# A two-layer encoder trunk on one core: the first norm's weights spread by a product with ones, and products that nobody reads ahead of the first real ones

## The chip, the core and the metric

The kernel runs on one core of a Trainium2 chip. A core has five engines that work side by side, each through its own queue and strictly in the order of that queue: TensorE (PE in the profile; its weight loads are shown as PEld), VectorE (DVE), ScalarE (ACT), GpSimd (POOL) and SyncE (SP, which here only issues DMAs). They wait for each other through semaphores. Matrix products read SBUF, the on-chip memory of 128 partitions, and write PSUM, from which VectorE or ScalarE take the results.

The metric is the device time of one execution, in microseconds (us); lower is better.

## What is computed

A float32 input of 512 tokens by 1024 features passes through two layers. Each layer is a token mixer and a channel mixer (a GeGLU network with a short convolution), each between two RMS norms:

```python
def rms_norm(x, g):
    xf = x.astype(jnp.float32)
    y = xf * lax.rsqrt(jnp.mean(xf * xf, axis=-1, keepdims=True) + EPS)
    return (y * g.astype(jnp.float32)).astype(x.dtype)
...
    for layer in range(DEPTH):
        i = layer // 2
        hn = rms_norm(x, norm_mix_pre[layer])
        if layer % 2 == 0:
            m = retention_na_mixer(hn, ab_w_in[i], ...)
        else:
            m = ssd_mixer(hn, c_w_in[i], ...)
        x = x + rms_norm(m, norm_mix_post[layer])
        f = conv_geglu_ffn(rms_norm(x, norm_ffn_pre[layer]), ...)
        x = x + rms_norm(f, norm_ffn_post[layer])
```

The change touches only the very first step, `rms_norm(x, norm_mix_pre[0])`, and what stands around it. The weights of that norm, `g`, are one row of 1024 numbers; the kernel needs them in every one of the 128 partitions.

## The kernel before

The 512 tokens are four tiles of 128 partitions (`t` = 0 to 3). The kernel is written with a framework that keeps pools of buffers, puts in the waits, and chooses each engine's order of instructions from the data dependences and from priorities; an engine then works its list off strictly in that order. So the place of an instruction in its engine's list matters as much as its inputs.

Start of the program (`trunk`): SP issues the loads of the four tiles of x (512 KB each), between them the load of the norm's weights and the first weight units of the mixer. The norm's weights come by `bcast` (L71): one DMA that writes the row of 4 KB into all 128 partitions, 512 KB in SBUF, called `gain`. Then for each tile t:

- `norm` (L113): ScalarE squares and sums the tile (`sumsq`, L110, written `junk`), VectorE adds the epsilon (`v_x`, L100), GpSimd raises to the power -1/2 (`r_x`, L102), and VectorE multiplies x by this and by `gain`, in two halves of 512 features (`xs`, L122).
- `turn` (L125): TensorE transposes each half in four products with the identity into one PSUM tile (`pt`, L131), and `split` (L77) takes it apart into a rounded part and the rest: ScalarE writes `xh` (L79), VectorE writes `xl` (L80).

Every product in the kernel is done as three (`mm3`, L82): rounded by rounded (L84), and the two cross terms with a rest (L85, L86). Weights are treated alike: `wunit` (L54) issues the load of a unit of 128 x 1024 into `wst` (two buffers), and `split` writes its rounded part `whi` on ScalarE (L79) and its rest `wlo` on VectorE (L80) into three buffers each. These splits are given a high priority, by which the framework places them early.

The first consumer, at the head of `mixer0`, is a projection: eight weight units, of which the first four make the first half; each unit serves two 128-row blocks of the contraction for each of the four token tiles, so one half has 4 x 4 x 2 x 3 = 96 products. The first product needs `xh` of tile 0 and the first `whi`; the second (L85) needs `xl` as well, the third (L86) `wlo`.

```python
                for t in range(NT):
                    tt = slice(t * P, (t + 1) * P)
                    for i in range(2):
                        k = 2 * u + i
                        E.mm3(ps[t], E.xh[:, k, tt], E.xl[:, k, tt], *w[i], k == 0, k == KD - 1)
```

PSUM has two pools of four tiles: `mm` for the sums of the projections, `px` for everything else, the transposes among it. A pool `tmp` of seven buffers holds, among others, `xs`.

Of the kernel before, what the change touches and what calls it, by code (L numbers as in the profile page):

```python
# [7 lines left out]
F32 = mybir.dt.float32  # L8
# [7 lines left out]
P = 128  # L16
S = 512
NT = S // P
D = 1024
# [6 lines left out]
class Env:  # L26


    def __init__(self, ctx, tc):
        self.tc, self.nc = tc, tc.nc  # L30
        nc = self.nc
        pool = lambda name, bufs, **kw: ctx.enter_context(tc.tile_pool(name=name, bufs=bufs, **kw))
        self.const = pool("const", 1)
        self.res = pool("res", 1)
        self.wst = pool("wst", 2)
        self.whi = pool("whi", 3)
        self.wlo = pool("wlo", 3)
        self.gain = pool("gain", 2)
        self.tmp = pool("tmp", 7)
        self.small = pool("small", 6)  # L40
        self.mm = pool("mm", 4, space=PSUM)
        self.px = pool("px", 4, space=PSUM)
        self.dram = pool("dram", 1, space=DRAM)

        self.ident = self.const.tile([P, P], F32, name="ident")
        make_identity(nc, self.ident)
        self.mhalf = self.const.tile([P, 1], F32, name="mhalf")
        nc.vector.memset(self.mhalf, -0.5)
        self.x = self.res.tile([P, NT, D], F32, name="x")
        self.xh = self.res.tile([P, KD, S], R32, name="xh")  # L50
        self.xl = self.res.tile([P, KD, S], R32, name="xl")
        self.late, self.xs = [], {}

    def wunit(self, src, parts=None):  # L54


        nc = self.nc
        st = self.wst.tile([P, 1024], F32, name="wst")
        nc.sync.dma_start(st, src)
        halves = slice(0, 512), slice(512, 1024)  # L60
        if parts is None:
            hi, lo = self.whi.tile([P, 1024], R32, name="whi"), self.wlo.tile([P, 1024], R32, name="wlo")
            with self.tc.high_priority(60):
                self.split(hi, lo, st)
            return [(hi[:, c], lo[:, c]) for c in halves]
        with self.tc.high_priority(60):
            for j, c in enumerate(halves):
                self.split(parts[j], parts[j + 2], st[:, c])
        return [(parts[j], parts[j + 2]) for j in range(2)]
# [789 lines left out]
def trunk(tc, x, norms, ab, ssd, ffns, out):  # L859

    nc = tc.nc
    with ExitStack() as ctx:
        E = Env(ctx, tc)
        w0 = []
        for t in range(NT):
            nc.sync.dma_start(E.x[:, t, :], x[t * P:(t + 1) * P])
            if t == 0:
                g0 = E.bcast(norms[0, 0])
            else:
                w0.append(E.wunit(ab[0][0, len(w0)]))  # L870
        for t in range(NT):
            E.norm(t, g0)
            E.turn(t)

        def then(row):
            g = []

            def done(t):
                if not g:
                    g.append(E.bcast(row))  # L880
                E.norm(t, g[0])
            return done

        def store(t):
            E.xs.pop(t, None)
            for h in range(2):
                c = slice(h * 512, h * 512 + 512)
                nc.sync.dma_start(out[t * P:(t + 1) * P, c], E.x[:, t, c])

        mixer0(E, w0, *ab, norms[0, 1], then(norms[0, 2]))  # L890
        ffn(E, *ffns[0], norms[0, 3], then(norms[1, 0]))
        mixer1(E, *ssd, norms[1, 1], then(norms[1, 2]))
        ffn(E, *ffns[1], norms[1, 3], store)
        E.flush()
# [80 lines left out]
def build(tc, ap, out):  # L975
    trunk(
        tc, ap["x"], ap["norms"],
        [ap["ab_" + n] for n in ("v", "fm", "rot", "dist", "logit", "gn", "bias", "out")],
        [ap["c_" + n] for n in ("dt", "fm", "cw", "dtc", "cols", "mask", "out")],
        [[ap[f"f{l}_{n}"] for n in ("up", "cw", "down")] for l in range(2)],  # L980
        out,
    )
# [18 lines left out]
```

## Time and profile before

| | us |
|---|---|
| median of 3 runs (lowest to highest) | 1478.65 (1475.88 to 1478.84) |
| time of the profiled execution | 1481.63 |
| its span, first to last instruction | 1479.9 |
| PE busy in it | 1445.4 (98%) |
| PEld busy | 1150.1 (78%) |
| DVE busy | 954.7 (65%) |
| ACT busy | 721.8 (49%) |
| POOL busy | 61.5 (4%) |

The profiled execution moved 166.34 MB by DMA, a mean of 112 GB/s. The mean granted TensorE clock of the span was 0.991 of full speed. Times in views are counted from the first instruction. A row of the timeline gives the start, the duration, the engine, the line of the program, the operation, the tile written and the tiles read, how many equal instructions are merged, and in brackets how long the engine was idle before and what ended that. Durations of neighbours on one engine overlap a little, since an instruction starts while the one ahead of it drains; the distance of two starts is what one of them costs in a row of many.

### The profile page before, as it was taken

What the parts mean: (1) busy time and instruction counts of PE and PEld (TensorE: products, weight loads), DVE (VectorE), ACT (ScalarE), POOL (GpSimd) and SP (SyncE); (2) the same over time, 40 slices, a digit from 0 to 9 for tenths busy, and PEclk for the clock granted to TensorE, in tenths of its full rate; (3) what the DMA queues carried; (4) which work ended last, traced back from release to release, by engine and by line L of the source; (5) the groups of instructions that cost most, each with busy time, mean ns of one, the idle gap of its engine ahead of it and who ended that gap; (6) DMA issues with size and microseconds to landing.
All of it is one profiled execution on the core that took longest, in us unless ns stands there. A gap on an engine that the chain in (4) does not pass through costs nothing.

```text
span 1479.9 us, 18034 instructions
## 1 busy us (share of the span) xinstructions
PE 1445.4 (98%) x6848; PEld 1150.1 (78%) x6848; DVE 954.7 (65%) x1484; ACT 721.8 (49%) x1186; POOL 61.5 (4%) x66
## 2 busy tenths in 40 slices
PE   7999999999999999999999999999899999999998
PEld 6866656788888888888778787777778888888886
DVE  7367668676665663236889886899887656654133
ACT  4345546445444442225688677567645444443121
POOL 0010100010000000001000000000020000000000
PEclk9999999999999999999999999999999999999999
DMA  7442132233333332242366355255532332333232
GB/s 247 150 129 77 51 100 65 74 101 93 92 101 100 92 101 84 93 127 98 110 176 202 107 164 160 70 151 155 173 111 86 100 100 89 100 97 100 85 100 85
DMA packets 56950, 166.34 MB, mean 112 GB/s; under 512 B 7200, under 2 KB 7968, under 8 KB 56864
## 3 DMA queue, kind: packets, MB, share of 16 engines
q1 hardware_dynamic: 56864, 165.20, 36.2%
q8 instruction: 54, 0.88, 0.2%
q14 instruction: 32, 0.26, 0.1%
HBM read 157.57 MB, written 5.51 MB: 110 GB/s over the span
## 4 chain that ended last, share of the span: by engine, by line
PE 82%; DVE 7%; DMA 4%; ACT 3%; issue 2%; POOL 1%; SPq 0%; DVEq 0%; POOLq 0%; ACTq 0%
PE mm L84 24%; PE mm L86 24%; PE mm L85 24%; DMA pb<-pd 2%; PE y L423 2%; DVE wlo L80 1%; DVE xf L654 1%; PE st L690 1%; PE sc L413 1%; PE pi L734 1%; PE pt L131 1%; DMA wst<-in_c_fm 1%; PE sc L412 1%; PE sc L458 1%; DMA wst<-in_c_out 1%
## 5 line engine op out<-in xcount | busy, mean ns | idle before, releaser
L84 PE MATMUL mm<-xh,whi 128*128 128x512 f32 (+2 forms) x1216 | 466.8, 384 | 2.4 <-DVE xf L654 1.4
L85 PE MATMUL mm<-xh,wlo 128*128 128x512 f32 (+2 forms) x1216 | 465.1, 383 | 0.7 <-DVE wlo L80 0.7
L86 PE MATMUL mm<-xl,whi 128*128 128x512 f32 (+2 forms) x1216 | 465.2, 383 | 0.0
L80 DVE TENSOR_TENSOR wlo<-wst,whi 128x1024 fp32r<-128x1024 f32 (+1 forms) x214 | 263.8, 1234 | 222.7 <-ACT whi L79 222.3
L79 ACT CAST whi<-wst 128x1024 fp32r<-128x1024 f32 (+1 forms) x214 | 223.4, 1044 | 218.4 <-PE mm L85 160.4
L84 PEld LDWEIGHTS mm<-xh,whi 128*128 128x128 f32 (+1 forms) x1216 | 229.3, 189 | 51.0 <-issue 4.1
L86 PEld LDWEIGHTS mm<-xl,whi 128*128 128x128 f32 (+1 forms) x1216 | 228.8, 188 | 47.3 <-issue 3.4
L85 PEld LDWEIGHTS mm<-xh,wlo 128*128 128x128 f32 (+1 forms) x1216 | 229.6, 189 | 45.4 <-issue 1.7
L216 DVE SCALAR_TENSOR_TENSOR cv<-mm,cwt,cv 128x511 f32<-128x511 f32 x88 | 65.7, 747 | 94.9 <-ACT cv L215 94.9
L84 PE MATMUL mm<-whi,hh 128*128 128x512 f32 x320 | 126.4, 395 | 0.0
L85 PE MATMUL mm<-whi,hl 128*128 128x512 f32 x320 | 126.3, 395 | 0.0
L86 PE MATMUL mm<-wlo,hh 128*128 128x512 f32 x320 | 126.3, 395 | 0.0
L215 ACT ACTIVATE cv<-mm,cwt 128x512 f32<-128x512 f32 x88 | 68.5, 778 | 38.1 <-PE mm L86 37.9
L79 ACT CAST hh<-cv 128x512 fp32r<-128x512 f32 x44 | 27.3, 621 | 100.2 <-DVE cv L224 100.0
L86 PEld LDWEIGHTS mm<-wlo,hh 128*128 128x128 f32 x320 | 60.3, 188 | 14.2
L85 PEld LDWEIGHTS mm<-whi,hl 128*128 128x128 f32 x320 | 60.3, 188 | 14.0
L84 PEld LDWEIGHTS mm<-whi,hh 128*128 128x128 f32 x320 | 60.3, 188 | 13.8
L222 ACT ACTIVATE cv<-cv 128x512 f32<-128x512 f32 x44 | 27.8, 632 | 86.3 <-DVE cv L217 86.3
L217 DVE SCALAR_TENSOR_TENSOR cv<-mm,cwt,cv 128x511 f32<-128x511 f32 x88 | 66.0, 750 | 3.0
L715 ACT ACTIVATE ds<-um,tok,ddt 128x128 f32<-128x128 f32 x128 | 55.7, 484 | 16.7 <-DVE e L718 16.3
L712 ACT ACTIVATE e<-pb,tok 128x128 f32<-128x128 f32 x128 | 42.8, 392 | 14.1 <-DMA pb<-pd 13.8
L654 DVE SCALAR_TENSOR_TENSOR xf<-mm,cwt,xf 128x510 f32<-128x510 f32 (+1 forms) x64 | 47.3, 742 | 3.5 <-ACT xf L651 3.4
(232 smaller groups left out, 1898.5 us busy)
## 6 DMA issues: line engine op xcount, KB each, us to landing
wst<-in_f_up SPq DMA_DIRECT2D x88, 512.0 KB
wst<-in_f_down SPq DMA_DIRECT2D x44, 512.0 KB
wst<-in_c_fm SPq DMA_DIRECT2D x40, 512.0 KB
pb<-pd SPq DMA_DIRECT2D x64, 256.0 KB
wst<-in_ab_fm SPq DMA_DIRECT2D x20, 512.0 KB
gain<-yd SPq DMA_DIRECT2D x32, 256.0 KB
wst<-in_c_out SPq DMA_DIRECT2D x16, 512.0 KB
gain<-in_norms SPq DMA_DIRECT2D x8, 512.0 KB
```

What stands on the lines that cost most here:

```text
L79: self.nc.scalar.copy(hi, src)
L80: self.nc.vector.tensor_tensor(lo, src, hi.bitcast(F32), op=ALU.subtract)
L84: mm(out, lh, rh, start=first, stop=False)
L85: mm(out, ll, rh, start=False, stop=False)
L86: mm(out, lh, rl, start=False, stop=last)
L215: nc.scalar.activation(o, ps, AF.Identity, scale=w(1), bias=w(3))
L216: nc.vector.scalar_tensor_tensor(o[:, 1:], ps[:, :S - 1], w(0), o[:, 1:], op0=ALU.mult, op1=ALU.add)
L217: nc.vector.scalar_tensor_tensor(o[:, :S - 1], ps[:, 1:], w(2), o[:, :S - 1], op0=ALU.mult, op1=ALU.add)
L423: nc.tensor.matmul(o["ry"][h * 64:h * 64 + 64], rv[:, i, c:c + 64], o["sd", i][h], start=i == 0, stop=i == NT - 1)
L654: nc.vector.scalar_tensor_tensor(r[:, a], ps[:, b], wc(j), r[:, a], op0=ALU.mult, op1=ALU.add)
L712: nc.scalar.activation(e[:, c], pb[0][:, cc], AF.Identity, scale=-1.0, bias=tok[:, 0, c, h:h + 1])
L715: nc.scalar.activation(ds[:, c], um, AF.Identity, scale=ddt[:, c, h:h + 1], bias=tok[:, 1, c, H + h:H + h + 1])
```

## The change

```diff
+    def lead_in(self, row):
+        nc = self.nc
+        one = self.const.tile([1, P], F32, name="one")
+        nc.vector.memset(one, 1.0)
+        src = [self.tmp.tile([1, 512], F32, name="row", tag="tmp") for _ in range(2)]
+        for h in range(2):
+            nc.sync.dma_start(src[h], row.rearrange("(o d) -> o d", o=1)[:, h * 512:h * 512 + 512])
+        idle = self.px.tile([P, P], F32, name="idle", tag="px")
+        for _ in range(8):
+            nc.tensor.matmul(idle, self.ident, self.ident, start=True, stop=True)
+        g = self.gain.tile([P, D], F32, name="gain")
+        for h in range(2):
+            c = slice(h * 512, h * 512 + 512)
+            ps = self.px.tile([P, 512], F32, name="pg", tag="px")
+            nc.tensor.matmul(ps, one, src[h], start=True, stop=True)
+            nc.scalar.copy(g[:, c], ps)
+        for _ in range(6):
+            nc.tensor.matmul(idle, self.ident, self.ident, start=True, stop=True)
+        return g
...
         w0 = []
+        g0 = E.lead_in(norms[0, 0])
         for t in range(NT):
             nc.sync.dma_start(E.x[:, t, :], x[t * P:(t + 1) * P])
-            if t == 0:
-                g0 = E.bcast(norms[0, 0])
-            else:
+            if t > 0:
                 w0.append(E.wunit(ab[0][0, len(w0)]))
```

The row of weights is now loaded into one partition, in two DMAs of 2 KB. A product of a column of ones with it (`pg`, one for each half) writes the row into all 128 partitions of PSUM, and ScalarE copies the two halves into `gain`. Ahead of these two products stand eight products of the identity with itself, behind them six, into a PSUM tile `idle` that is never read. All sixteen are plain float32 products. The 512 KB broadcast DMA is gone. The other norms of the kernel still use `bcast`.

The framework then orders all instructions anew. Line numbers of the program move by 22 (L79 becomes L101, L122 becomes L144). Behind the first projection every engine's list is as before; at the start it is not. The first rows of ScalarE's list, before (`junk` with `ssx` is the sum of squares, one instruction for each tile):

```order
L110 ACT_TABLE_LOAD
L110 ACTIVATE junk,ssx<-x 128x1024 x2
L79 CAST whi<-wst 128x1024
L79 CAST xh<-pt 128x4x128 x2
L110 ACTIVATE junk,ssx<-x 128x1024
L79 CAST whi<-wst 128x1024
```

and of the change:

```order
L132 ACT_TABLE_LOAD
L132 ACTIVATE junk,ssx<-x 128x1024
L101 CAST whi<-wst 128x1024 x2
L71 COPY gain<-pg 128x512 x2
L132 ACTIVATE junk,ssx<-x 128x1024
L101 CAST whi<-wst 128x1024
L101 CAST xh<-pt 128x4x128 x3
```

The two copies that make `gain` stand behind the casts of the first two weight units, and the sum of squares of the second tile stands behind those copies.

VectorE's list from its first work on x, before:

```order
L100 TENSOR_SCALAR v_x<-ssx 128x1
L122 SCALAR_TENSOR_TENSOR xs<-x,r_x,gain 128x512 x2
L100 TENSOR_SCALAR v_x<-ssx 128x1
L122 SCALAR_TENSOR_TENSOR xs<-x,r_x,gain 128x512 x2
L80 TENSOR_TENSOR wlo<-wst,whi 128x1024
L80 TENSOR_TENSOR xl<-pt,xh 128x4x128 x2
```

and of the change:

```order
L122 TENSOR_SCALAR v_x<-ssx 128x1
L102 TENSOR_TENSOR wlo<-wst,whi 128x1024 x2
L144 SCALAR_TENSOR_TENSOR xs<-x,r_x,gain 128x512 x2
L122 TENSOR_SCALAR v_x<-ssx 128x1
L144 SCALAR_TENSOR_TENSOR xs<-x,r_x,gain 128x512 x2
L102 TENSOR_TENSOR wlo<-wst,whi 128x1024
L102 TENSOR_TENSOR xl<-pt,xh 128x4x128 x4
```

The rests of the first two weight units now stand ahead of the first `xs`, and that of the third unit ahead of the first `xl`.

TensorE's list from its start, of the change; before, it began with the sixteen transposes of tiles 0 and 1, and the products L84, L85, L86 behind them:

```order
L65 MATMUL idle<-ident 128x128 x8
L70 MATMUL pg<-row,one 128x512 x2
L73 MATMUL idle<-ident 128x128 x6
L153 MATMUL pt<-ident,xs 128x128 x12
L106 MATMUL mm<-whi,xh 128x512
L153 MATMUL pt<-ident,xs 128x128 x4
L106 MATMUL mm<-whi,xh 128x512
L107 MATMUL mm<-whi,xl 128x512
```

The lead-in stands ahead of all transposes, and two products of the first kind now come ahead of the first with `xl` (L107; before, L85).

SP's list, the issues of the first loads, before:

```order
L866 DMA x<-in_x 128x1024
L74 DMA gain<-in_norms 128x1024
L866 DMA x<-in_x 128x1024
L59 DMA wst<-in_ab_v 128x1024
L866 DMA x<-in_x 128x1024
L59 DMA wst<-in_ab_v 128x1024
L866 DMA x<-in_x 128x1024
```

and of the change:

```order
L62 DMA row<-in_norms 1x512 x2
L889 DMA x<-in_x 128x1024 x2
L81 DMA wst<-in_ab_v 128x1024
L889 DMA x<-in_x 128x1024
L81 DMA wst<-in_ab_v 128x1024
L889 DMA x<-in_x 128x1024
L81 DMA wst<-in_ab_v 128x1024
```

The second weight unit was the sixth transfer of 512 KB and is now the fifth; the two short rows are issued ahead of x.

## The prediction

> **What bounds the kernel now.** I read the page first, to see which engine sets the end, then the chain of waits over the start, then the timelines of single engines there, since the change touches nothing behind the first projection.
>
> ```profile
> PE 1445.4 (98%) x6848; PEld 1150.1 (78%) x6848; DVE 954.7 (65%) x1484; ACT 721.8 (49%) x1186; POOL 61.5 (4%) x66
> ...
> 24.00:28.00 4.00, 3.99 (x20) 3.13 (x19) 3.31 (x14) 1.99 (x3) 0.00 (x0) 1.00 0.46 172
> 28.00:32.00 4.00, 4.00 (x19) 3.33 (x18) 3.86 (x9) 1.05 (x1) 0.00 (x0) 1.00 0.45 129
> ```
>
> TensorE is busy for 98% of the span, and in the two stretches of 4 us (first number behind the comma) for all of it. So what happens before TensorE runs without a break is paid once, in full, and every microsecond by which that point moves should move the end. The chain of waits names what leads there:
>
> ```profile
> 1.64 6.04 DMA x<-in_x
> 7.71 1.16 ACT junk L110 x2
> 9.12 0.56 POOL r_x L102
> 9.71 0.76 DVE xs L122
> 10.52 1.97 PE pt L131 x8
> 12.49 0.43 PE mm L84
> 12.91 0.79 PE mm L85
> ```
>
> The second tile of x lands, is squared, scaled and transposed, and the products start. The **marker** I use is the first product with `xl` (L85): it starts at 12.91, and from there TensorE has no gap. It begins slowly:
>
> ```profile
> 14.36 0.63 PE L85 MATMUL mm<-whi,xl 128*128 128x512 f32 x1
> 14.79 0.63 PE L86 MATMUL mm<-wlo,xh 128*128 128x512 f32 x1
> ...
> 16.92 0.42 PE L84 MATMUL mm<-whi,xh 128*128 128x512 f32 x1
> ...
> 22.44 0.39 PE L85 MATMUL mm<-whi,xl 128*128 128x512 f32 x1
> 22.66 0.39 PE L86 MATMUL mm<-wlo,xh 128*128 128x512 f32 x1
> ```
>
> Two products start 0.43 us apart at first, and 0.22 to 0.23 after 16.92: half the clock until then. (The clock column shows 1.00 there too; it shows no half before its first recorded change, so the distance of starts decides.) Between marker and rise lie 4.0 us, some 9 products, which lose about 0.2 us each: **1.9 us** is all that a warm clock could give here.
>
> **The change part by part.** The new lists of ScalarE and VectorE decide. `gain` is copied on ScalarE behind the casts of the first two weight units, and `xs` of tile 0 stands on VectorE behind the rests of both. Both engines hold their order, so the first `xs`, which ran at 6.56, now waits until the **second weight unit** has landed and been split. These are the rows that price the new chain:
>
> ```profile
> 4.56 1.06 ACT L110 ACTIVATE junk<-x 128x1024 bf16<-128x1024 f32 x1 [2.54 <-DMA x<-in_x]
> 7.71 1.06 ACT L110 ACTIVATE junk<-x 128x1024 bf16<-128x1024 f32 x1 [2.00 <-DMA x<-in_x]
> ...
> 11.94 1.04 ACT L79 CAST whi<-wst 128x1024 fp32r<-128x1024 f32 x1
> ...
> 16.02 1.05 ACT L79 CAST whi<-wst 128x1024 fp32r<-128x1024 f32 x1 [2.06 <-DMA wst<-in_ab_v]
> ```
>
> ```profile
> 6.56 1.42 DVE L122 SCALAR_TENSOR_TENSOR xs<-x,r_x,gain 128x512 f32<-128x512 f32 x2 [0.67 <-POOL r_x L102]
> 8.89 0.15 DVE L100 TENSOR_SCALAR v_x<-ssx 128x1 f32<-128x1 f32 x1 [0.91 <-ACT junk L110]
> 9.71 1.42 DVE L122 SCALAR_TENSOR_TENSOR xs<-x,r_x,gain 128x512 f32<-128x512 f32 x2 [0.67 <-POOL r_x L102]
> 11.04 1.22 DVE L80 TENSOR_TENSOR wlo<-wst,whi 128x1024 fp32r<-128x1024 f32 x1
> 12.18 1.28 DVE L80 TENSOR_TENSOR xl<-pt,xh 128x512 fp32r<-128x512 f32 x2
> ```
>
> ```profile
> 0.74 0.39 SPq L866 DMA_DIRECT2D x<-in_x  x1
> 1.19 0.41 SPq L74 DMA_DIRECT2D gain<-in_norms  x1
> 1.64 0.43 SPq L866 DMA_DIRECT2D x<-in_x  x1
> ...
> 6.00:8.00 2.00, 0.63 (x3) 0.63 (x4) 1.42 (x2) 0.29 (x1) 0.53 (x1) 1.00 1.02 418
> 8.00:10.00 2.00, 1.34 (x7) 0.94 (x5) 0.44 (x2) 1.87 (x4) 0.55 (x1) 1.00 1.04 424
> 10.00:12.00 2.00, 1.48 (x7) 1.49 (x8) 2.00 (x3) 2.00 (x6) 0.00 (x0) 1.00 1.01 412
> ```
>
> *When the second unit lands.* Before, the third transfer of 512 KB (tile 1) landed at 7.71, where ScalarE stopped waiting for it. The last number of the three windows is GB/s: at 418, 512 KB take 1.25 us, so the fifth transfer landed near 10.2, and the second unit, then the sixth, near 11.5. Now it is the fifth. Against it, two short rows are issued first, 0.45 us each (0.74, 1.19, 1.64): x goes out 0.9 later. Upper end: 10.2 + 0.9 = 11.1. Lower end: the third transfer came 3.15 us after the first (7.71 - 4.56), 0.65 more than two at full rate; if that was the broadcast's doing and the rows delay nothing, it is 9.55. With the delay and without the slow spell, 10.45. I take **10.6**, near the middle of the last and the upper end.
>
> *From there, step by step.* The cast of the unit takes 1.05: 11.65. Its rest on VectorE takes 1.22: 12.87. Beside it ScalarE makes the two copies of `gain`. This trace has no copy of `pg`; the nearest row is another copy of 128x512 out of PSUM:
>
> ```profile
> L336 ACT COPY nv<-mm 128x512 f32<-128x512 f32 x4 | 2.3, 586 | 2.1 <-PE mm L86 2.1
> ```
>
> Two of these end at 12.8, just beside the rest. If they cost double, the first half is still there in time; the second delays half of `xs` by some 0.5. Then `xs` of tile 0, 1.42: 14.3. The sum of squares of tile 1 on ScalarE follows the copies and ends at 14.05, so it is hidden. `v_x` to `xs` through GpSimd took 9.71 - 8.89 = 0.82: 15.1. `xs` of tile 1, 1.33 to the next start: 16.45. The third unit's rest, 1.14 to the next start: 17.6. Then the first `xl`; in the trace from its start to the marker 12.91 - 12.18 = 0.73. The marker comes at **18.3**.
>
> The third unit hides, but not by much. Its load may be issued when the first unit's rest is done (about 10.3); the trace's third unit was issued at 12.29 and cast at 16.02, 3.7 later, so near 14.0, and its cast behind the sum of squares ends at 15.1, before VectorE wants it at 16.45. Without this 1.35 of cover it would add to the chain.
>
> *The lead-in on TensorE* costs nothing by itself. The trace has no such products; the nearest are plain float32 products of the same sizes, each of which is recorded as two:
>
> ```profile
> L679 PE MATMUL pg<-cf,bf 128*128 128x128 f32 x32 | 4.2, 275 | 0.0
> L431 PE MATMUL var<-sq,bones 128*128 128x512 f32 x8 | 4.3, 618 | 0.0
> ```
>
> By these, at full clock, one of the identity's takes 0.26 us and one of `pg` 1.1; at half clock double. All sixteen take 5.8 to 11.7 us from 1.3 on, when the identity is made. They end by 13.0, and the first transpose cannot start before half of `xs`, 13.6. The copies need `pg` by 11.65; it is done by 10 even at half clock. The cover is the wait for the second unit; without it these products would stand in front of x.
>
> *Sum.* The marker moves from 12.91 to 18.3: +5.4. One product more is done ahead of it, -0.43. Transposes left (sixteen) and products left (but one) are the same. Behind the marker I checked the last half of tile 3 on VectorE, the tightest input: it should be ready at 26.7, and TensorE, still beginning at half clock, reaches its transposes near 27.4. So **+5.0 us** reach the end: 1481.63 + 5.0 = 1486.6 against the profiled execution. That one stands 3.0 above the median of the runs; against the median, **1483.7**.
>
> **Does the warm-up hold?** TensorE ends the lead-in between 7 and 10 us if the clock rises in it, and then has nothing to do until 13.6. What a pause does is seen later in the trace (busy time of PE, then of the other engines; third number from the end is the granted clock):
>
> ```profile
> 1064.84:1068.25 3.41, 1.09 (x16) 0.88 (x16) 2.57 (x6) 3.00 (x7) 0.00 (x0) 1.00 0.76 265
> 1068.25:1071.66 3.41, 3.13 (x18) 2.10 (x18) 3.41 (x5) 2.58 (x4) 1.82 (x1) 0.50 0.66 187
> ```
>
> After 3.41 us with PE busy for 1.09, the next 3.41 run at half clock. A pause of 3.6 us or more should therefore undo the lead-in, and the products begin at 0.43 as before; the sum takes it so. [...]
>
> **The rivals.**
>
> *The warmth lasts until the products.* Against it speak the two rows and the length of the pause; for it, that the pause is short if the lead-in runs at half clock throughout. Then the 13 products behind the marker cost 0.23 instead of 0.43, 2.6 less, but TensorE would soon wait for VectorE's `xs` of tile 3, ready near 26.1 where the forecast uses it at 27.4: 1.3 less. +3.7, 1482.4. Chance 0.08. [...]
>
> *The half-clock stretches fall elsewhere* (the case that is not slower). The clock is set in steps of 3.41 us, and a stretch of weakly used products costs a step or not by where the steps fall:
>
> ```profile
> 88.63:92.04 3.41, 3.41 (x9) 1.48 (x9) 3.18 (x6) 3.33 (x5) 0.00 (x0) 1.00 0.39 144
> 92.04:95.45 3.41, 3.41 (x9) 2.07 (x10) 2.06 (x4) 2.58 (x3) 0.00 (x0) 0.50 0.15 10
> ...
> 1102.39:1105.80 3.41, 3.41 (x16) 3.05 (x15) 3.38 (x8) 1.79 (x4) 0.00 (x0) 0.50 0.62 202
> ```
>
> Here 9 products in a step cost the next one. There are seven such stretches (at 92, 143, 194, 826, 1068, 1082 and 1102 us; the first and the last are shown), each worth half of 3.41, 1.7. The program slides by 5 us, so they are drawn anew. Three fewer undo the forecast (-5.1, 1478.6); two fewer leave 1480.3, within the bound; five fewer make it faster. The spread of the runs before, 3 us, is of that size. Chance of two or more fewer: 0.18; of two more (1487.1): 0.08.
>
> *The second unit lands so early that the new order does not matter.* To leave the marker's place unchanged it would have to land 5.0 us earlier, at 5.6. The first transfer alone landed at 4.56, and four more at 1.25 follow. I give it 0.01.
>
> **How the numbers follow.** The forecast has 0.65, with a range of its own of 1481.7 to 1486.5: the landing between 9.55 and 11.1 (-1.05, +0.5); the slow start, 4.0 us before, between 3.4 and 6.8 by where the steps of 3.41 fall, at 0.47 lost of each (-0.3, +1.3); one half-clock stretch more or less (1.7). With the rivals 8 times in 10 lie between 1480.3 (two stretches fewer) and 1487.7 (two more, with half a microsecond of landing). A measurement of this kernel tells about 0.2%, 3.0 us, from no change. Above 1481.6 lie most of the forecast, the lasting warmth and the extra stretches: 0.80. Within 0.2% lie the forecast's lowest end and two or three stretches fewer: 0.16. Faster needs five fewer: 0.04.
>
> **What would show it.** In the profile of the changed kernel: ScalarE idle before its second cast of `whi` until that unit lands near 10.6; the copies of `gain` at 11.6 to 12.8; the first `xs` behind two `wlo` at 12.9 and not near 7; TensorE idle for 3 us or more between the last idle product and the first transpose; the first L107 near 18.3, and products 0.43 us apart for 3.4 to 6.8 us behind it. I would be wrong if `xs` of tile 0 started before 11, if the products started 0.23 apart at once, or if the marker moved by 5 us and the end did not: then the loss was given back at a later wait or in the half-clock stretches.

## The result, and the profile after

The changed kernel is slower: median 1482.47 us (22 runs) against 1476.45 us (22 runs of the kernel before, on the same chips). The ratio is 1.0034, with a 95% interval of 1.0019 to 1.0048; of 1476.45 us that is +5.0 us, between 2.8 and 7.1. The ratio is not the quotient of the two medians, which differ by 6.0 us. Of all runs in this document one, of the kernel without the unread products below, took 2035.12 us at a granted clock of 0.655; the ratios leave it out.

The timelines of ScalarE and of VectorE in the changed kernel show the start (the first number is the start, the second the duration, in brackets the idle time ahead and what ended it):

```profile
10.60 1.04 ACT L101 CAST whi<-wst 128x1024 fp32r<-128x1024 f32 x1 [1.51 <-DMA wst<-in_ab_v]
11.55 1.06 ACT L71 COPY gain<-pg 128x512 f32<-128x512 f32 x2
...
14.13 1.04 ACT L101 CAST whi<-wst 128x1024 fp32r<-128x1024 f32 x1 [0.47 <-DMA wst<-in_ab_v]
```

```profile
11.68 1.23 DVE L102 TENSOR_TENSOR wlo<-wst,whi 128x1024 fp32r<-128x1024 f32 x1 [1.34 <-ACT whi L101]
12.82 1.41 DVE L144 SCALAR_TENSOR_TENSOR xs<-x,r_x,gain 128x512 f32<-128x512 f32 x2
...
16.29 1.22 DVE L102 TENSOR_TENSOR wlo<-wst,whi 128x1024 fp32r<-128x1024 f32 x1
```

ScalarE waits at 10.60 for the second weight unit, with `pg` long finished; the copies of `gain` come behind that cast, and the first `xs` starts at 12.82, where it stood at 6.56 before. The chain of waits goes the same way (start, duration, what):

```profile
3.23 7.34 DMA wst<-in_ab_v
10.60 1.05 ACT whi L101
...
12.82 0.91 DVE xs L144 x2
```

TensorE's timeline there:

```profile
1.36 3.78 PE L65 MATMUL idle<-ident 128*128 128x128 f32 x16 [1.36 <-POOL ident masks.py:199]
5.07 3.78 PE L70 MATMUL pg<-row,one 1*128 1x512 f32 x4
8.78 2.93 PE L73 MATMUL idle<-ident 128*128 128x128 f32 x12
13.62 1.97 PE L153 MATMUL pt<-ident,xs 128*128 128x128 f32 x8 [1.92 <-DVE xs L144]
...
18.16 0.50 PE L107 MATMUL mm<-whi,xl 128*128 128x512 f32 x1
18.50 0.40 PE L108 MATMUL mm<-wlo,xh 128*128 128x512 f32 x1
18.74 0.39 PE L106 MATMUL mm<-whi,xh 128*128 128x512 f32 x1
...
21.02 0.39 PE L108 MATMUL mm<-wlo,xh 128*128 128x512 f32 x1
21.53 0.63 PE L153 MATMUL pt<-ident,xs 128*128 128x128 f32 x4
...
23.14 0.62 PE L106 MATMUL mm<-whi,xh 128*128 128x512 f32 x2
24.25 0.63 PE L153 MATMUL pt<-ident,xs 128*128 128x128 f32 x4 [0.49 <-DVE xs L144]
```

The lead-in ends at 11.7 and TensorE waits for `xs`. The marker, the first L107, is at 18.16. The next product starts 0.34 us behind it, and from there two products start 0.23 to 0.24 us apart: full clock at once. But between 21.02 and 24.25 TensorE has to wait twice for VectorE's `xs` of the later tiles.

What this costs is read off behind the first projection, at one and the same instruction of both kernels. I take the `wlo` of VectorE that starts near 45 us. Before and after:

```profile
45.15 1.23 DVE L80 TENSOR_TENSOR wlo<-wst,whi 128x1024 fp32r<-128x1024 f32 x1 [2.89 <-ACT whi L79]
```

```profile
48.98 1.23 DVE L102 TENSOR_TENSOR wlo<-wst,whi 128x1024 fp32r<-128x1024 f32 x1 [3.32 <-ACT whi L101]
```

The profiled execution of the changed kernel is **3.83 us** late there. It is still 3.7 late at 300 us:

```profile
298.07 0.15 DVE L100 TENSOR_SCALAR v_x<-ssx 128x1 f32<-128x1 f32 x1 [1.28 <-ACT junk L110]
```

```profile
301.76 0.15 DVE L122 TENSOR_SCALAR v_x<-ssx 128x1 f32<-128x1 f32 x1 [1.28 <-ACT junk L132]
```

At the end it is 1.9 late (spans 1481.8 and 1479.9). The difference behind 300 us is one stretch at half clock fewer, as the windows over 1050 to 1120 us show (the third number from the end is the granted clock), before and then after:

```profile
1050.00:1120.00 70.00, 61.30 (x354) 50.75 (x353) 59.45 (x99) 36.53 (x69) 11.73 (x12) 0.93 0.41 126
```

```profile
1050.00:1120.00 70.00, 61.41 (x357) 50.61 (x356) 61.10 (x104) 37.79 (x73) 11.71 (x12) 0.95 0.41 132
```

0.02 of 70 us is 1.4 us. Behind the first rise and up to 1110 us, the clock recorded in the trace has seven steps of 3.41 us at half clock before, and six after. How much of the time runs at half clock changes from one execution to the next: in 23 runs of the kernel before, the granted clock lies between 0.987 and 0.997 and the time between 1470.78 and 1485.14 us. So two profiles may differ by several microseconds at the end where the medians agree. In what follows the time at this `wlo` tells what a start costs, and the ratio of many runs tells whether it reaches the end.

### The profile page after: what moved, and what is told of

Same layout as the page of the kernel before. It is cut to its first block, busy times and chain, and to the rows that moved or that the text cites. A ratio compares the mean times of both kernels' runs of the same rounds, so it can differ in the third digit from the quotient of the medians.

```text
span 1481.8 us, 18106 instructions
## 1 busy us (share of the span) xinstructions
PE 1451.8 (98%) x6880; PEld 1154.1 (78%) x6880; DVE 954.5 (64%) x1485; ACT 722.9 (49%) x1188; POOL 61.7 (4%) x66
## 4 chain that ended last, share of the span: by engine, by line
PE 82%; DVE 7%; DMA 4%; ACT 4%; issue 2%; POOL 1%; SPq 0%; DVEq 0%; POOLq 0%; ACTq 0%
PE mm L106 24%; PE mm L108 24%; PE mm L107 24%; DMA pb<-pd 2%; PE y L445 2%; PE st L712 1%; DVE wlo L102 1%; PE sc L435 1%; DVE xf L676 1%; PE sc L434 1%; ACT ds L737 1%; PE pi L756 1%; DVE xs L144 1%; PE sc L480 1%; ACT e L734 1%
## 5 line engine op out<-in xcount | busy, mean ns | idle before, releaser
L107 PE MATMUL mm<-xh,wlo 128*128 128x512 f32 (+2 forms) x1216 | 464.8, 382 | 0.7 <-DVE wlo L102 0.7
L101 ACT CAST whi<-wst 128x1024 fp32r<-128x1024 f32 (+1 forms) x214 | 223.5, 1045 | 222.2 <-PE mm L107 163.5
L107 PEld LDWEIGHTS mm<-xh,wlo 128*128 128x128 f32 (+1 forms) x1216 | 228.9, 188 | 46.0 <-issue 1.7
L107 PE MATMUL mm<-whi,hl 128*128 128x512 f32 x320 | 126.3, 395 | 0.0
L101 ACT CAST hh<-cv 128x512 fp32r<-128x512 f32 x44 | 27.3, 621 | 100.2 <-DVE cv L246 99.9
L107 PEld LDWEIGHTS mm<-whi,hl 128*128 128x128 f32 x320 | 60.3, 188 | 14.0
```

The source lines that it names most:

```text
L101: self.nc.scalar.copy(hi, src)
L107: mm(out, ll, rh, start=False, stop=False)
```

## The experiments

The theory: the unread products cost nothing as work; they make the framework list `pg` and the copies of `gain` late, and the 4 to 5 us come from that order alone. The rivals: the products themselves stand in the way, or the exchange of the broadcast for `row` and `pg` is what costs. Line numbers differ a little between these kernels; names don't. Each edit is against the changed kernel.

### Without the unread products

```diff
-        idle = self.px.tile([P, P], F32, name="idle", tag="px")
-        for _ in range(8):
-            nc.tensor.matmul(idle, self.ident, self.ident, start=True, stop=True)
...
-        for _ in range(6):
-            nc.tensor.matmul(idle, self.ident, self.ident, start=True, stop=True)
```

> The changed kernel without its fourteen unread products: the row, the two products with ones and the two copies stay. Without the eight products ahead of `pg` the framework puts the copies of `gain` first on ScalarE and `xs` of tile 0 ahead of every `wlo` on VectorE. Theory (the order on ScalarE and VectorE is the whole loss): the first product with `xl` starts near 11.8 us and not at 18.2 as in the changed kernel, and instructions behind the first projection start 0 to 2 us earlier than before the change, not 3.8 us later; ratio to before 0.998 to 1.000. Rival (the loss comes from spreading the row by a product and two copies, or from x being issued behind the rows): they stay 3 us or more later, ratio 1.002 or more.

Measured: ratio 1.0006, interval 0.9986 to 1.0026 (median 1475.07 us against 1476.85). The framework's list for ScalarE now has the copies first:

```
1 L68 ACT_TABLE_LOAD
2 L68 COPY gain<-pg 128x512 x2
3 L127 ACTIVATE junk,ssx<-x 128x1024
4 L96 CAST whi<-wst 128x1024
```

From its timelines of TensorE, ScalarE and VectorE, in order of time, with the `wlo` near 45 us last:

```profile
2.16 3.75 PE L67 MATMUL pg<-row,one 1*128 1x512 f32 x4 [2.16 <-DMA row<-in_norms]
...
4.24 0.58 ACT L68 COPY gain<-pg 128x512 f32<-128x512 f32 x1 [2.22 <-PE pg L67]
...
8.44 1.42 DVE L139 SCALAR_TENSOR_TENSOR xs<-x,r_x,gain 128x512 f32<-128x512 f32 x2 [0.67 <-POOL r_x L119]
...
12.03 0.79 PE L102 MATMUL mm<-whi,xl 128*128 128x512 f32 x1
...
44.92 1.23 DVE L97 TENSOR_TENSOR wlo<-wst,whi 128x1024 fp32r<-128x1024 f32 x1 [2.81 <-ACT whi L96]
```

`pg` starts at 2.16, as soon as the row is there, the copies follow it (the first at 4.24), and the first `xs` waits for the norm's own chain, no longer for a weight unit. The marker comes at 12.03, where 11.8 was expected, and behind the first projection this kernel is 0.23 us ahead of the kernel before. So the exchange of the broadcast for `row`, `pg` and two copies costs nothing that can be told, and gains nothing; the loss came with the unread products. The ratio stands a little above the 0.998 to 1.000 that was expected, and its interval holds nearly all of these values; the medians differ by 1.8 us the other way, within the noise.

That its profiled span is 7.9 us shorter (1472.0) is in the main again the half-clock stretches. The first of three windows of 60 us before, and the same without the products (the other two, up to 240 us, have the same clocks, 0.97 and 1.00):

```profile
60.00:120.00 60.00, 60.00 (x237) 40.81 (x235) 34.28 (x66) 26.89 (x47) 4.40 (x3) 0.97 0.43 136
```

```profile
60.00:120.00 60.00, 60.00 (x243) 41.32 (x242) 36.00 (x69) 28.70 (x51) 4.68 (x3) 1.00 0.41 136
```

One stretch of 3.41 us at half clock makes 0.97 of 60 us; three, one in each of these windows, are missing in this execution, and at 300 us it is 4.7 us ahead where it was 0.23 ahead at 45. The ratio doesn't follow it, so this is the draw of one execution and no merit of the kernel.

### The eight products ahead of `pg` alone, and all fourteen behind it

```diff
-        for _ in range(6):
+        for _ in range(0):
             nc.tensor.matmul(idle, self.ident, self.ident, start=True, stop=True)
         return g
```

> The changed kernel with only the eight unread products ahead of `pg`, without the six behind it. ScalarE's and VectorE's lists are those of the change. Theory (order): behind the first projection everything starts 3.8 us later than before the change, as in the changed kernel (3.5 to 4.2), since the six products ran in TensorE's idle time. Rival (products that nobody reads cost TensorE time themselves): at least 1 us less than 3.8.

```diff
-        for _ in range(8):
+        for _ in range(0):
...
-        for _ in range(6):
+        for _ in range(14):
```

> The changed kernel with all fourteen unread products behind `pg` instead of eight ahead and six behind. `gain` is copied first and `xs` of tile 0 stands ahead of `wlo` again, but the products now stand between `pg` and the first transpose: at half clock 14 x 0.47 = 6.5 us from about 6 to 12.4 us. Theory: `xs` of tile 0 starts near 8.6, the transposes only near 12.4, the first product with `xl` near 16, and behind the projection 1.5 to 3 us are lost instead of 3.8. Rival (the unread products warm the clock once nothing waits for them): the clock rises before 12.4 us and no more than 1 us is lost.

Measured: eight ahead, ratio 1.0027 (1.0006 to 1.0048); fourteen behind, 0.9983 (0.9965 to 1.0002). The first `wlo` row is of the kernel with eight ahead, the second of that with fourteen behind:

```profile
48.66 1.23 DVE L102 TENSOR_TENSOR wlo<-wst,whi 128x1024 fp32r<-128x1024 f32 x1 [3.33 <-ACT whi L101]
```

```profile
44.24 1.22 DVE L102 TENSOR_TENSOR wlo<-wst,whi 128x1024 fp32r<-128x1024 f32 x1 [3.12 <-ACT whi L101]
```

Eight products ahead of `pg` are late by 3.51 us, nearly all of the loss, and leave `gain` behind two casts. The same fourteen products behind `pg` are *early* by 0.91 us: the list then has the copies first, as without any products. Not the number of unread products decides, but whether they stand ahead of `pg`. Here the theory lost a part: I expected fourteen behind `pg` to hold the transposes until 12.4 and to cost 1.5 to 3 us. They do hold them, until 11.62 (9.24 without any), but the rival holds, since the clock rises meanwhile. TensorE with fourteen behind:

```profile
5.87 5.91 PE L73 MATMUL idle<-ident 128*128 128x128 f32 x28
11.62 1.65 PE L153 MATMUL pt<-ident,xs 128*128 128x128 f32 x12
```

At half clock 16 of these records take 3.78 us (the changed kernel, 1.36) and start 0.21 apart, so 28 would take 6.3. They took 5.9: the last four or so ran at full clock, which came near 11.2, and all behind them runs at that clock.

### Twenty bfloat16 products behind `pg`

```diff
+        idle = self.px.tile([P, 512], F32, name="idle", tag="px")
+        wide = self.const.tile([P, 512], BF16, name="wide")
+        nc.vector.memset(wide, 0.5)
...
+        for _ in range(20):
+            nc.tensor.matmul(idle, wide[:, :P], wide, start=True, stop=True)
```

> The changed kernel, its fourteen float32 products replaced by twenty bfloat16 products of 128x128 with 128x512 (of a constant 0.5) behind `pg`; one look for the clock. Rival A (products that go through the array once release the clock, plain float32 ones do not): starts are 0.43 us apart at first and 0.22 from some point between 9 and 13 us. Rival B (the clock is held down for about the first 17 us of the program whatever runs): 0.43 apart to the end of the twenty, near 14.5 us, and full clock only near 17.

One execution: 1473.1 us. The unread products on TensorE's timeline, and the `wlo`:

```profile
5.86 7.01 PE L73 MATMUL idle<-wide 128*128 128x512 bf16 x20
...
47.23 1.22 DVE L102 TENSOR_TENSOR wlo<-wst,whi 128x1024 fp32r<-128x1024 f32 x1 [2.89 <-ACT whi L101]
```

The first twelve start 0.43 us apart and the last eight 0.22 to 0.23, from 11.01. So in these two executions float32 products of the identity (from 5.87 on, rise near 11.2) and bfloat16 products (from 5.86 on, rise at 11.01) raised the clock alike; the type isn't what kept the lead-in of the changed kernel cold. These twenty are too many: they hold the transposes until 12.7, VectorE, whose list now has the first `xl` ahead of the `xs` of tile 1, stands idle for 2.9 us ahead of 13.97, and the kernel is 2.08 us late at the `wlo`.

### The order of the changed kernel, without unread products

The copies of `gain` are made to wait for the rounded second weight unit: each is multiplied by a column that is computed as that unit times 0 plus 1.

```diff
-            nc.scalar.copy(g[:, c], ps)
+            self.gain_parts = getattr(self, "gain_parts", []) + [(g[:, c], ps)]
...
+    def gain_late(self, w):
+        nc = self.nc
+        col = self.const.tile([P, 1], F32, name="col")
+        nc.scalar.activation(col, w.bitcast(F32)[:, :1], AF.Identity, scale=0.0, bias=self.onecol)
+        for g, ps in self.gain_parts:
+            nc.scalar.activation(g, ps, AF.Identity, scale=col)
```

The fourteen products are left out as in the first experiment.

> No unread products at all, but the copies of `gain` take a scale of 1 that is read off the second weight unit's `whi` (times 0, plus 1), so they stand behind two casts on ScalarE, and two `wlo` stand ahead of `xs` of tile 0 on VectorE, as in the changed kernel. Theory (order alone): the first product with `xl` near 18.5 us, everything behind the first projection 3.5 to 5 us later than before the change, ratio 1.002 to 1.004. Rival (the unread products are part of the loss): less than 2 us later, since without them the same row, product and copies lost nothing.

Measured: ratio 1.0053, interval 1.0031 to 1.0075 (median 1484.29 against 1475.42 us). From its timelines of the three engines, in order of time:

```profile
11.98 1.26 ACT L78 ACTIVATE gain<-pg,col 128x512 f32<-128x512 f32 x2
...
12.79 1.41 DVE L148 SCALAR_TENSOR_TENSOR xs<-x,r_x,gain 128x512 f32<-128x512 f32 x2
...
13.59 1.97 PE L157 MATMUL pt<-ident,xs 128*128 128x128 f32 x8 [7.60 <-DVE xs L148]
...
16.03 1.70 PE L157 MATMUL pt<-ident,xs 128*128 128x128 f32 x8 [0.47 <-ACT xh L105]
...
18.34 0.50 PE L111 MATMUL mm<-whi,xl 128*128 128x512 f32 x1
...
49.38 1.23 DVE L106 TENSOR_TENSOR wlo<-wst,whi 128x1024 fp32r<-128x1024 f32 x1 [3.33 <-ACT whi L105]
```

First `xs` at 12.79, marker at 18.34 and 4.23 us late at the `wlo`: with the order alone, and not one unread product, everything that the changed kernel lost is there (12.82, 18.16, 3.83). The ratio is above the 1.002 to 1.004 that was expected, with a part of that inside its interval. Together with the first two experiments this settles the cause.

### Eight products behind `pg`, as a better version

```diff
-        for _ in range(8):
+        for _ in range(0):
...
-        for _ in range(6):
+        for _ in range(8):
```

> The candidate for a faster kernel: `pg` first, then eight unread products, none ahead. They should end near 9.6 us, when the first half of `xs` is ready, so they stand in nobody's way, and fill at least one step of 3.41 us. If that raises the clock (near 9 to 13 us), the products behind begin at 0.23: 1 to 2.5 us earlier than before the change behind the first projection. If not, within 0.5 us of the kernel without unread products (0.2 earlier than before). The ratio cannot tell either from no change: 0.998 to 1.000.

Measured: ratio 1.0003, interval 0.9979 to 1.0027 (median 1475.48 against 1475.42 us). Its marker is the earliest of all; at the `wlo` it is level with fourteen behind `pg` (44.24). The timelines of TensorE and, for the last row, VectorE:

```profile
5.85 3.39 PE L73 MATMUL idle<-ident 128*128 128x128 f32 x16
9.25 1.38 PE L153 MATMUL pt<-ident,xs 128*128 128x128 f32 x8
...
11.71 0.50 PE L107 MATMUL mm<-whi,xl 128*128 128x512 f32 x1 [0.62 <-DVE xl L102]
...
17.22 0.63 PE L153 MATMUL pt<-ident,xs 128*128 128x128 f32 x4 [0.41 <-DVE xs L144]
...
44.22 1.23 DVE L102 TENSOR_TENSOR wlo<-wst,whi 128x1024 fp32r<-128x1024 f32 x1 [2.79 <-ACT whi L101]
```

The sixteen records take 3.39 us, not 3.78: the clock rises near 8.7. All products run at full clock (behind the marker they start 0.23 to 0.24 us apart), and the marker comes 1.2 us before that of the kernel before. But the warm TensorE now waits for VectorE (0.62 at the marker, 0.41 at 17.22), and 0.93 us is left at the `wlo`, a little less than the 1 to 2.5 expected. That is 0.06% of the time and can't be told from nothing. Of it 0.23 is there without any unread product (44.92), so the eight are worth 0.70 us. Here the clock rose 6.5 us behind the first product, which was a `pg` (2.17), and 2.84 us behind the first of the eight; so the warm-up worked as far as the clock goes, and is worth these 0.7 us. No version was found that is measurably faster than the kernel before.

### Each product of `pg` four times

```diff
-            nc.tensor.matmul(ps, one, src[h], start=True, stop=True)
+            for _ in range(4):
+                nc.tensor.matmul(ps, one, src[h], start=True, stop=True)
```

The unread products are left out.

> One look at the clock: no identity products, but each of the two products with ones (one row of the array in use) done four times, 8 x 1.87 = 15 us at half clock from 2.2 us on without a gap. Theory (a product with one active row does not count as work for the clock): starts of the recorded halves stay 0.93 apart to the end near 17, no rise in that time. Rival (any running product counts): the rise comes by 9 us and the starts halve.

One execution: 1483.91 us. TensorE's timeline:

```profile
2.23 13.99 PE L68 MATMUL pg<-row,one 1*128 1x512 f32 x16 [2.23 <-DMA row<-in_norms]
...
21.09 0.40 PE L104 MATMUL mm<-wlo,xh 128*128 128x512 f32 x1
21.33 0.40 PE L102 MATMUL mm<-whi,xh 128*128 128x512 f32 x1
```

Fourteen microseconds of these products without a gap left the clock at half: sixteen records take 13.99 us, some 0.87 each, where a warm `pg` takes 2.09 for four, 0.52 each (in the last section). The rise comes at 21.1, 4.9 us behind the first transpose (16.15). So in this one execution products that use one row of the array, as `pg` does (`1*128` in the row), did not raise the clock in 14 us.

## Why the prediction held, and which term was off

The forecast was +5.0 us, 1483.7 us; measured are +5.0 by the ratio (2.8 to 7.1), with a median of 1482.47 us. The order and the waits came as forecast. That the +5.0 is met to the digit is luck in part: the profiled execution pays 3.8, and the 1483.7 stood on a median of three runs before, 1478.65, where 22 runs gave 1476.45. By its steps:

- **The second weight unit** lands and is cast at 10.60; 10.6 was taken. Its parts were less exact and made up for each other: the first x was issued 0.67 us later and not 0.9 (1.41 against 0.74), its square sum began 0.58 later (5.14 against 4.56), and the second unit came 5.46 behind that, where four transfers at the rate before (1.25 us each at 418 GB/s) would have taken 5.0.
- **The copies** run from 11.55 to 12.6 beside the second `wlo`, and the first `xs` starts at 12.82; 11.6 to 12.8 and 12.9 were forecast. The copies take 0.53 us each, near the 0.59 of the row that priced them.
- **The third unit hides**: its cast starts at 14.13, and `wlo` takes it on VectorE at 16.29, where 16.45 was expected.
- **The marker** comes at 18.16, forecast 18.3. It moved by 5.25 us. The forecast took off 0.43 for the one product more ahead of it; with a slow start as long as before, as the forecast had it, one product fewer saves only 0.23, so its sum should have been +5.2.
- **The lead-in costs nothing by itself**: with it and without it, in the same order, the marker is at 18.16 and 18.34.
- **What failed in size is the slow start behind the marker.** The forecast let the products start 0.43 us apart for 3.4 to 6.8 us from the marker on, as long as before, so that nothing of the 1.9 us came off. In the profile they start at full clock, which the forecast itself had named as a sign of being wrong. The clock rises at 17.47, 0.7 us ahead of the marker and 3.85 us behind the first transpose, from which TensorE has work with short breaks. In the forced order, with no lead-in at all, it comes at 17.34, 3.75 us behind its first transpose; so it isn't the lead-in's doing. With eight ahead it comes at 18.99, 5.7 us behind (13.31); what sets this distance was not shown. Before, the transposes of tile 0 and tile 1 had a pause between them, and the rise fell 4.0 us behind the marker, 6.4 behind the transposes of tile 1:

```profile
10.52 1.97 PE L131 MATMUL pt<-ident,xs 128*128 128x128 f32 x8 [1.18 <-DVE xs L122]
```

From the rows the sum for the profiled execution is then 5.25 - 0.23 - 1.9 for the slow start that is gone, + 0.93 for the two waits on `xs` (21.53 is 0.28 later than a start 0.23 behind 21.02, and 24.25 is 0.65 later than two such steps behind 23.14), - 0.26 for a wait that the kernel before had there (a product started 0.61 behind the transposes at 23.79, where 0.35 is usual) = 3.79; the `wlo` shows 3.83. This is the price, +3.7, of the rival "the warmth lasts until the products", with its step that TensorE then waits for VectorE, but not with its reason: the lead-in ran at half clock from end to end (its 28 records took 6.7 us) and warmed nothing. That the marker moves by 5 us and the end does not was another sign that the forecast had named; in the profiled execution the end moved by 1.9, over the runs by 2.8 to 7.1.

How often an execution begins so can't be read from one profile of each kernel. The interval of the ratio holds 3.8 as well as 5.0 us, so the runs don't tell the two sums apart.

The rival "half-clock stretches fall elsewhere" is real, as one stretch fewer in the profiled execution shows, but over the runs it didn't undo the loss. The rival that the second unit lands early has no support.

## What to carry to other kernels

Products added only to warm TensorE are also entries for the scheduler: ahead of a product that others wait for, they can push its consumers behind other work on other engines, and that order, not the products, cost 4 us here. Look at each engine's list after such an edit, and put the filler behind the work that feeds the path. Then weigh what a warm start can give at all: here 0.7 us, since VectorE was next.

## What the runs showed of the hardware that was not expected

**The clock stayed at half under 14 us of products with one row** (above, one execution). The lead-in of the changed kernel, whose `pg` products (5.07 to 8.78) stand between 3.7 and 2.9 us of the identity's, didn't raise it either. With eight ahead and none behind, the same eight products of the identity, from 1.36 on as there, did raise it (below); why in the one execution and not in the other was not shown.

**How long the clock took to rise differed.** For each of the nine profiled executions, the start of TensorE's first work other than `pg`, and the first rise, by the recorded clock and by the distances of starts in the rows:

| kernel | first work but `pg`, us | rise, us | later by, us |
|---|---|---|---|
| eight behind `pg` | 5.85, identity | 8.69 | 2.8 |
| forced order | 13.59, transposes | 17.34 | 3.8 |
| eight ahead of `pg` | 1.36, identity | 5.33 | 4.0 |
| each `pg` four times | 16.15, transposes | 21.1 | 4.9 |
| twenty bfloat16 | 5.86, bfloat16 | 11.01 | 5.2 |
| fourteen behind `pg` | 5.87, identity | 11.2 | 5.3 |
| without unread products | 9.24, transposes | 15.84 | 6.6 |
| before | 7.37, transposes | 16.95 | 9.6 |
| changed | 1.36, identity | 17.47 | 16.1 |

In the three longest of these, TensorE's work ahead of the rise has breaks: in the changed kernel `pg`, and a wait of 1.92 us ahead of 13.62; before, a wait of 1.18 us ahead of 10.52; without unread products, starts at 11.30, 12.03 and 12.62, 0.73 and 0.59 us apart where 0.43 is usual. What sets the time was not shown.

**The clock rose behind transposes alone.** In the forced order TensorE did nothing but transposes between `pg`, which ended at 6.0, and its first product at 17.48, and the clock rose at 17.34.

**The full clock lasted 3.41 us.** With eight ahead and none behind, the clock rose at 5.3, as the `pg` products began. TensorE's timeline of that kernel, and two windows of 3.41 us each (third number from the end: granted clock):

```profile
5.07 2.09 PE L70 MATMUL pg<-row,one 1*128 1x512 f32 x4
13.31 1.97 PE L153 MATMUL pt<-ident,xs 128*128 128x128 f32 x8 [6.16 <-DVE xs L144]
```

```profile
5.33:8.74 3.41, 1.82 (x4) 0.51 (x4) 0.15 (x1) 1.98 (x3) 0.55 (x1) 1.00 1.03 418
8.74:12.15 3.41, 0.00 (x0) 0.00 (x0) 2.01 (x2) 1.90 (x4) 0.00 (x0) 0.50 0.83 324
```

`pg` took 2.09 us in place of 3.78, but the clock fell at 8.74, 3.41 us behind the rise and 1.6 us into the pause; in these 3.41 us TensorE did only `pg`, for 1.82 us. The transposes at 13.31 take 1.97, the half-clock figure (1.04 for the same eight in the kernel with twenty bfloat16 products), and the clock rose again only at 18.98. As the forecast had it from the later rows, this warm-up came too early: it was gone 4.6 us ahead of the first transpose.

**Open:** why the clock stayed at half under 14 us of `pg`, and whether it was the one row in use or something else in `pg` (its 512 columns in plain float32). Such products of more rows were not tried.
